# One ring of four two-bank PSUM tiles in the first attention, and each head's output in its own half of the array

## The chip, the cores and the metric

The kernel runs on one core of a Trainium2 chip. The metric is the device time of one launch in microseconds (us). Before the change it is 3492.91 us (median of three runs, 3492.39 to 3498.04).

The engines have short names in the profile: PE is TensorE's matmuls, PEld its weight loads, DVE VectorE, ACT ScalarE, POOL GpSimd, SP the engine that issues the DMAs. PSUM is TensorE's output memory: eight banks, each 512 float32 columns over 128 partitions.

## The reference

One inference step of two layers, each an attention and a squared-ReLU MLP, for a prompt of 1024 tokens and for 8 samples of 8 new tokens with paged caches. The change concerns the first attention over the prompt. Cut to what matters (16 query heads of 64 channels share 2 key/value heads; three branches: compressed rows, all earlier rows, the last 512 rows):

```python
s = jnp.einsum('btkgd,bckd->bkgtc', qg, kc)               # compressed: at most 64 columns
p_cmp = softmax(where(c_ok, s, NEG)); o_cmp = einsum('bkgtc,bckd->btkgd', p_cmp, vc)
...                                                        # selected: top 16 of 16 blocks, causal
p = softmax(where(ok, s, NEG)); o_sel = einsum('bkgtnj,bktnjd->btkgd', p, vg)
s = jnp.einsum('btkgd,bckd->bkgtc', qg, kw)               # window: the last 512 rows
p = softmax(where(ok_w, s, NEG)); o_win = einsum('bkgtc,bckd->btkgd', p, vw)
g = gates.reshape(B, Tq, Hk, G, 3)
out = o_cmp * g[..., 0:1] + o_sel * g[..., 1:2] + o_win * g[..., 2:3]
```

## The kernel before

The stage is the method `nsa_prompt`. It works on 8 pairs of heads `p`, and in each pair on 8 block rows `i` of 128 queries, in the order 0, 7, 1, 6, 2, 5, 3, 4. A unit (p, i) has two parts.

`scores(p, i)` computes for each of the two heads the scores of the three branches with float32 matmuls into PSUM tiles `S` of two banks (one tile for i below 3, else two), takes each branch's maximum on VectorE (L675), exponentiates on ScalarE into an SBUF tile `P` (L678, the last reader of `S`), takes a reciprocal (L682) and scales `P` by reciprocal and gate on GpSimd (L685).

`values(p, i)` multiplies `P` by the values. The product contracts over keys, so each block of 128 columns of `P` is first transposed on TensorE (L109), for both heads, into a PSUM tile `tr` of one bank that holds two blocks of both heads; one copy per tile, alternately on VectorE and ScalarE (the call at L714, recorded at L98 and L96), moves it to the SBUF tile `PT`. A block row has 3, 5, 7, 9, 11, 12, 13 or 14 blocks (i = 0 to 7), 74 per pair. The value matmuls (L726, recorded at L106) use 64 of the 128 columns of the array: a matmul takes one block's values as weights and streams both heads' 256 columns, and successive blocks go to the lower and the upper half of the array, which accumulate in the two halves of the partitions of a tile `av` of [128, 256]. So the two halves hold two partial sums: ScalarE copies the lower one to `oh` (L729), and VectorE adds the upper one, a head at a time (L731), into `oT`. A float32 matmul is recorded as two passes; "x24" in a row are 24 such records.

`prep(p+1)` transposes the queries of the next pair (L625) and splits them into two parts (`X`).

The PSUM tiles come from three pools of two (L614): `Sp` 2 x 2 banks, `trp` 2 x 1, `avp` 2 x 1, eight banks in all. A pool gives its tiles in turn; a tile's first writer waits until the last reader of the tile that had its place is done, and instructions on one tile wait for each other as far as they are of different engines and at least one writes.

The generators of all units are run in an interleaved order set by `stagger`, from start and length given for each at the end of the function (`ng` is the number of steps of `values`); every engine then runs its instructions in program order.

Of the kernel before, what the change touches and what calls it, by code (L numbers as in the profile page):

```python
# [12 lines left out]
AF = mybir.ActivationFunctionType  # L13
OP = mybir.AluOpType
AX = mybir.AxisListType
PSUM = bass.MemoryType.PSUM
# [55 lines left out]
class Step:  # L72
# [534 lines left out]
    def nsa_prompt(self, oT):  # L607
        nc, io = self.nc, self.io
        cmN, A, B, V = self.cmN, self.A, self.B, self.V
        with ExitStack() as ctx:  # L610

            qp = self.pool(ctx, bufs=2, side="right")
            sp = self.pool(ctx)
            Sp, trp, avp = (self.pool(ctx, bufs=2, space=PSUM) for _ in range(3))  # L614
            st = {}

            def prep(p):
                k = p // 4
                X = [(sp if p % 2 else qp)("X", [128, NP], F32R, bufs=2) for _ in range(2)]
                st[p] = X  # L620
                qn = qp("qn", [128, 8, 128])
                nc.sync.dma_start(qn, self.zq[0:NP, p * 128:p * 128 + 128].rearrange("(t p) c -> p t c", p=128))
                for g in range(2):
                    cs = slice(g * 512, g * 512 + 512)
                    ps = trp("tr", [128, 512]) if p else Sp("S", [128, 1024])[:, 0:512]  # L625
                    for i in range(4):
                        self.tr(ps[:, i * 128:i * 128 + 128], qn[:, 4 * g + i, :], 128)
                    for s in range(2):
                        self.qk_prep(ps, s * 64, X[s][k * 64:k * 64 + 64, cs], X[s][64 - k * 64:128 - k * 64, cs])
                        yield  # L630
# [59 lines left out]
            def scores(p, i):  # L690
                for s in range(2):
                    yield from score(p, i, s)

            def values(p, i):


                k = p // 4
                ks = slice(k * 64, k * 64 + 64)
                P, w1, j0 = zip(*(st[p, i, s] for s in range(2)))
                w1, j0 = w1[0], j0[0]  # L700

                blocks = [(0, V[0][:, ks])]
                blocks += [(64 + j * 128, V[1][:, j, ks]) for j in range(i + 1)]
                blocks += [(64 + w1 + (j - j0) * 128, V[2][:, j, ks]) for j in range(j0, i + 1)]
                nb = len(blocks)
                PT = sp("PT", [128, 14, 2, 128], bufs=2)
                for x0, x1 in [(max(x, 0), x + 2) for x in range(-(nb % 2), nb, 2)]:
                    ps = trp("tr", [128, 2, 2, 128])
                    for x in range(x0, x1):
                        for s in range(2):  # L710
                            o = blocks[x][0]
                            last = self.tr(ps[:, x - x0, s], P[s][:, o:o + 128], 128)
                    self.n_p += 1
                    self.hi("va"[self.n_p % 2], PT[:, x0:x1], ps[:, 0:x1 - x0])  # L714
                    yield
                av = avp("av", [128, 256])
                todo = [(x, None) for x in range(nb - 1, nb % 2 - 1, -1)] + [(0, s) for s in range(2) if nb % 2]
                with self.tc.issue_after(last.ins):
                    for c, (x, s) in enumerate(todo):
                        h = slice(c % 2 * 64, c % 2 * 64 + 64)  # L720
                        y = PT[:, x] if s is None else PT[:, x, s]
                        if s is None:
                            o, y = av[h], y.rearrange("p a b -> p (a b)")
                        else:
                            o = av[h, s * 128:s * 128 + 128]
                        self.mm(o, blocks[x][1], y, c < 2, c >= len(todo) - 2)  # L726
                yield
                oh = sp("oh", [64, 256], bufs=2)
                nc.scalar.activation(oh, av[0:64], AF.Copy)  # L729
                for s in range(2):  # L730
                    nc.vector.tensor_tensor(oT[p][s * 64:s * 64 + 64, i * 128:i * 128 + 128],  # L731
                                            av[64:128, s * 128:s * 128 + 128], oh[:, s * 128:s * 128 + 128], OP.add)

            units = [(p, i) for p in range(8) for i in (0, 7, 1, 6, 2, 5, 3, 4)]
            gens = [(-1, 1, 4, prep(0))] + [(8 * p + 0.5, 7, 4, prep(p + 1)) for p in range(7)]
            for u, (p, i) in enumerate(units):
                ng = (i + 1 + min(i + 1, 5) + 2) // 2
                gens.append((u, 1, 4 if i < 3 else 8, scores(p, i)))
                gens.append((u + 1.2, 1, ng + 1, values(p, i)))
            stagger(gens)  # L740
# [813 lines left out]
```

## Time and profile before

| | |
|---|---|
| median of three runs | 3492.91 us |
| the profiled execution | 3498.1 us, its span 3496.3 us |
| mean granted clock of TensorE over the span | 0.986 |
| the stage `nsa_prompt` | from 480.8 to about 1011 us of the span, 65.3 us per pair |
| TensorE busy in 476 to 1012 us | 499.9 of 536 us |
| VectorE, ScalarE, GpSimd busy there | 361.9, 355.0, 246.8 us |

A row of the groups reads: source line, engine, operation, output<-input by the program's names, shapes, count | busy us, mean ns of one | idle time of the engine just before, and what ended it. A helper that all stages share has one line: L106 is the matmul, L109 the transposition, L96 and L98 the copies on ScalarE and VectorE. A matmul's recorded duration includes the time until its last column is out; the step from one start to the next is the rate.

### The profile page before, as it was taken

The numbers are of one execution on the slowest core, as the hardware profiler recorded it, in microseconds if no ns is written. First come the engines' busy times: TensorE is split into PE (matmuls) and PEld (weight loads), VectorE is DVE, ScalarE is ACT, GpSimd is POOL, SyncE is SP. The second block draws the span as 40 slices with busy tenths as digits, with TensorE's granted clock in tenths as the row PEclk, the third lists the DMA queues.
The fourth block names the chain that finished last, engine by engine and source line by source line (L and its number), as shares of the span: only waits on it lengthen the run. The fifth ranks groups of instructions, "written<-read, shape, count | busy, mean of one in ns | idle before, by whom it ended". The sixth has DMA issues, their size and how long they took to land.

```text
span 3496.3 us, 57244 instructions
## 1 busy us (share of the span) xinstructions
PE 3361.6 (96%) x21901; PEld 2827.9 (81%) x21901; DVE 1934.7 (55%) x4109; ACT 1233.5 (35%) x3084; POOL 746.2 (21%) x1036
## 2 busy tenths in 40 slices
PE   7999989999999999999999999899989999999998
PEld 5879756666679999999998777667669999999998
DVE  4356566766665444445447213777775544444445
ACT  6223466666653111111114221667763211111111
POOL 0242234444430011100004203222230100111102
PEclk9999999999999999999999999999999999999999
DMA  7433420000012111111113222666631211111111
GB/s 222 146 91 98 139 64 7 7 13 1 1 65 75 34 49 49 49 43 43 36 37 116 94 94 89 216 220 224 203 100 56 60 49 31 49 49 49 43 37 52
DMA packets 242380, 270.88 MB, mean 77 GB/s; under 512 B 23930, under 2 KB 190970, under 8 KB 242042
## 3 DMA queue, kind: packets, MB, share of 16 engines
q1 hardware_dynamic: 242106, 267.23, 24.4%
q8 instruction: 172, 2.82, 0.3%
q14 instruction: 102, 0.84, 0.1%
HBM read 229.81 MB, written 41.50 MB: 78 GB/s over the span
## 4 chain that ended last, share of the span: by engine, by line
PE 83%; DVE 6%; ACT 5%; DMA 2%; SPq 2%; issue 1%; POOL 0%; DVEq 0%; ACTq 0%; POOLq 0%
PE dn L106 26%; PE up L106 22%; PE ps L106 12%; PE av L106 7%; PE S L106 6%; PE tr L109 6%; PE hid L106 2%; ACT P L678 2%; PE tr L106 1%; DVE ml L675 1%; SPq L142 1%; DVE PT L98 1%; DVE hl L242 0%; DVE oT L103 0%; DVE oT L731 0%
## 5 line engine op out<-in xcount | busy, mean ns | idle before, releaser
L1061 DVE TENSOR_TENSOR xT<-xT,dn 128x512 f32<-128x512 f32 (+2 forms) x768 | 404.0, 530 | 497.5 <-PE dn L106 496.6
L106 PE MATMUL dn<-xh,dh 128*128 128x512 f32 (+2 forms) x1536 | 504.5, 328 | 0.6 <-DVE xT L1061 0.6
L106 PE MATMUL up<-hh,uh 128*128 128x512 f32 (+2 forms) x1536 | 503.9, 328 | 1.2 <-DVE u L1037 1.2
L106 PE MATMUL dn<-xl,dh 128*128 128x512 f32 (+2 forms) x1536 | 504.7, 329 | 0.0
L106 PE MATMUL dn<-xh,dl 128*128 128x512 f32 (+2 forms) x1536 | 503.4, 328 | 0.0
L106 PE MATMUL up<-hh,ul 128*128 128x512 f32 (+2 forms) x1536 | 502.8, 327 | 0.0
L106 PE MATMUL up<-hl,uh 128*128 128x512 f32 (+2 forms) x1536 | 502.4, 327 | 0.0
L99 POOL TENSOR_SCALAR xh<-u 128x512 fp32r<-128x512 f32 (+2 forms) x192 | 142.8, 744 | 1309.5 <-PE dn L106 858.6
L1038 ACT ACTIVATE u<-u 128x512 f32<-128x512 f32 (+2 forms) x192 | 96.5, 502 | 829.3 <-DVE u L1037 827.3
L106 PEld LDWEIGHTS up<-hh,uh 128*128 128x128 f32 x1536 | 289.7, 189 | 25.1 <-DVE u L1037 1.8
L106 PEld LDWEIGHTS up<-hl,uh 128*128 128x128 f32 x1536 | 289.7, 189 | 22.3
L106 PEld LDWEIGHTS up<-hh,ul 128*128 128x128 f32 x1536 | 289.6, 189 | 22.2
L106 PEld LDWEIGHTS dn<-xh,dh 128*128 128x128 f32 x1536 | 289.5, 188 | 21.5 <-DVE xT L1061 1.0
L106 PEld LDWEIGHTS dn<-xh,dl 128*128 128x128 f32 x1536 | 289.2, 188 | 21.6
L106 PEld LDWEIGHTS dn<-xl,dh 128*128 128x128 f32 x1536 | 289.5, 188 | 19.9
L685 POOL TENSOR_SCALAR P<-P,ml,gates 128x64 f32<-128x64 f32 (+8 forms) x384 | 244.5, 652 | 281.8 <-DVE ml L682 254.8
L106 PE MATMUL ps<-wh,hh 128*128 128x512 f32 (+2 forms) x720 | 278.7, 388 | 9.5 <-ACT wh L96 7.4
L106 PE MATMUL S<-A,X 128*128 128x512 f32 (+7 forms) x608 | 250.5, 412 | 29.4 <-ACT P L678 22.4
L106 PE MATMUL ps<-wh,hl 128*128 128x512 f32 (+2 forms) x720 | 277.5, 387 | 0.0
L106 PE MATMUL ps<-wl,hh 128*128 128x512 f32 (+2 forms) x720 | 277.4, 386 | 0.1
L109 PE MATMUL tr<-ident,P 128*128 128x128 f32 (+1 forms) x1584 | 245.9, 282 | 19.4 <-DVE PT L98 6.8
L678 ACT ACTIVATE P<-S,ml 128x64 f32<-128x64 f32 (+8 forms) x384 | 216.3, 571 | 84.1 <-DVE ml L675 65.0
(311 smaller groups left out, 6386.4 us busy)
## 6 DMA issues: line engine op xcount, KB each, us to landing
ur<-in_mlp_w_up_dram SPq DMA_DIRECT2D x64, 512.0 KB
dr<-in_mlp_w_down_dram SPq DMA_DIRECT2D x64, 512.0 KB
kt<-in_cache_diff_kv_dram SPq DMA_DIRECT2D x64, 512.0 KB
vt<-in_cache_diff_kv_dram SPq DMA_DIRECT2D x64, 512.0 KB
ur<-in_diff_w_in_dram SPq DMA_DIRECT2D x24, 512.0 KB
xT<-x_saved SPq DMA_DIRECT2D x16, 544.0 KB
nat<-in_cache_nsa_cmp_dram SPq DMA_DIRECT2D x128, 64.0 KB
zq<-ro SPq DMA_DIRECT2D x32, 256.0 KB
```

The source lines that it names most:

```text
L98: return self.nc.vector.tensor_copy(out, x)
L99: return self.nc.gpsimd.tensor_scalar(out, x, 1.0, 0.0, op0=OP.mult, op1=OP.add)
L106: self.nc.tensor.matmul(out, lhsT, rhs, start=start, stop=stop)
L109: return self.nc.tensor.transpose(out, x, self.ident[:n, :n])
L142: self.page_dmas.append(self.nc.sync.dma_start(out, in_))
L675: nc.vector.tensor_reduce(nm[:, br:br + 1], x, AX.X, OP.max, negate=True)
L678: nc.scalar.activation(P[:, c:c + x.shape[1]], x, AF.Exp, bias=nm[:, br:br + 1], accum_out=l[:, br:br + 1])
L685: nc.gpsimd.tensor_scalar(P[:, c0:c1], P[:, c0:c1], l[:, br:br + 1], g[:, br:br + 1], op0=OP.mult, op1=OP.mult)
L1038: nc.scalar.activation(u[:, :w], u[:, :w], AF.Square)
L1061: nc.vector.tensor_tensor(x, x, ps[:, :w], OP.add)
```

## The change

The three pools become one, `Sp`, a ring of four tiles of two banks. Out of it come, in program order, the score tiles, the query transpositions of `prep`, the transpositions of `values`, and the outputs.

- A transposition tile holds four blocks of both heads, one pair of blocks in each bank; each bank has its copy as before.
- The output tile is [128, 128]: the product of head 0 goes to the lower, that of head 1 to the upper half of the array, each with 128 streamed columns per block and all blocks accumulated in the one half. One VectorE copy of 128x128 moves it to `oT`. `oh`, its ScalarE copy and the two additions are gone.
- `ng` counts groups of four blocks now.

```diff
-            Sp, trp, avp = (self.pool(ctx, bufs=2, space=PSUM) for _ in range(3))
+
+            Sp = self.pool(ctx, bufs=4, space=PSUM)
...
-                    ps = trp("tr", [128, 512]) if p else Sp("S", [128, 1024])[:, 0:512]
+                    ps = Sp("S", [128, 1024])[:, 0:512]
...
-                for x0, x1 in [(max(x, 0), x + 2) for x in range(-(nb % 2), nb, 2)]:
-                    ps = trp("tr", [128, 2, 2, 128])
-                    for x in range(x0, x1):
+                for x0 in range(0, nb, 4):
+                    ps = Sp("S", [128, 1024]).rearrange("p (x s c) -> p x s c", x=4, s=2)
+                    for y0 in range(x0, min(x0 + 4, nb), 2):
+                        y1 = min(y0 + 2, nb)
+                        for x in range(y0, y1):
+                            for s in range(2):
+                                o = blocks[x][0]
+                                last = self.tr(ps[:, x - x0, s], P[s][:, o:o + 128], 128)
+                        self.n_p += 1
+                        self.hi("va"[self.n_p % 2], PT[:, y0:y1], ps[:, y0 - x0:y1 - x0])
+                    yield
+                av = Sp("S", [128, 1024])[:, 0:128]
+                with self.tc.issue_after(last.ins):
+                    for x in range(nb - 1, -1, -1):
                         for s in range(2):
-                            o = blocks[x][0]
-                            last = self.tr(ps[:, x - x0, s], P[s][:, o:o + 128], 128)
-                    self.n_p += 1
-                    self.hi("va"[self.n_p % 2], PT[:, x0:x1], ps[:, 0:x1 - x0])
-                    yield
-                av = avp("av", [128, 256])
-                todo = [(x, None) for x in range(nb - 1, nb % 2 - 1, -1)] + [(0, s) for s in range(2) if nb % 2]
-                with self.tc.issue_after(last.ins):
-                    for c, (x, s) in enumerate(todo):
-                        h = slice(c % 2 * 64, c % 2 * 64 + 64)
...
-                        self.mm(o, blocks[x][1], y, c < 2, c >= len(todo) - 2)
+                            self.mm(av[s * 64:s * 64 + 64], blocks[x][1], PT[:, x, s], x == nb - 1, x == 0)
+                nc.vector.tensor_copy(oT[p][:, i * 128:i * 128 + 128], av)
                 yield
-                oh = sp("oh", [64, 256], bufs=2)
-                nc.scalar.activation(oh, av[0:64], AF.Copy)
-                for s in range(2):
-                    nc.vector.tensor_tensor(oT[p][s * 64:s * 64 + 64, i * 128:i * 128 + 128],
-                                            av[64:128, s * 128:s * 128 + 128], oh[:, s * 128:s * 128 + 128], OP.add)
...
-                ng = (i + 1 + min(i + 1, 5) + 2) // 2
+                ng = (i + 1 + min(i + 1, 5) + 1 + 3) // 4
```

Place 1 is TensorE's order at block row 7 of the second pair: the end of its scores and its transpositions (`tr<-ident,P` before, `S<-ident,P` after, since the tiles come from the ring; the name in brackets is the engine waited for). Before:

```order
L109 MATMUL tr<-ident,P 128x128 [waits Activation_49]
L109 MATMUL tr<-ident,P 128x128 x3
L106 MATMUL S<-A_6227,X 128x512 [waits Activation_49]
L106 MATMUL S<-B_6228,X 128x512
L106 LDWEIGHTS identb
L106 MATMUL S<-masks,identb 128x128
L106 MATMUL S<-A_6227,X 128x128
L106 MATMUL S<-B_6228,X 128x128
L106 LDWEIGHTS identb
L106 MATMUL S<-masks,identb 128x128
L109 MATMUL tr<-ident,P 128x128 [waits DVE_49]
L109 MATMUL tr<-ident,P 128x128 x3
```

After:

```order
L109 MATMUL S<-ident,P 128x128 [waits Pool_49]
L109 MATMUL S<-ident,P 128x128 x7
L109 MATMUL S<-ident,P 128x128 [waits Pool_49]
L109 MATMUL S<-ident,P 128x128 [waits PE_49,Activation_49]
L109 MATMUL S<-ident,P 128x128 x3
L109 MATMUL S<-ident,P 128x128 [waits Activation_49]
L109 MATMUL S<-ident,P 128x128 x3
L109 MATMUL S<-ident,P 128x128 [waits Activation_49]
L109 MATMUL S<-ident,P 128x128 x3
L109 MATMUL S<-ident,P 128x128 [waits Activation_49]
L109 MATMUL S<-ident,P 128x128 x3
L106 MATMUL S<-A_5690,X 128x512 [waits DVE_49]
```

Before, groups of four transpositions stand between score tiles. After, the first halves of four tiles and then the second halves of three stand together, each second half behind a wait for ScalarE, and the next score tile behind a wait for VectorE.

Place 2 is TensorE's order at block row 2 of the second pair (7 blocks), from its last transpositions to its value products; the numbers are those of the buffers. Before:

```order
L109 MATMUL tr_7963<-ident_65,P_7850 128x128 [waits DVE_49,Pool_49]
L109 MATMUL tr_7963<-ident_65,P_7902 128x128 [waits Pool_49]
L109 MATMUL tr_7963<-ident_65,P_7850 128x128
L109 MATMUL tr_7963<-ident_65,P_7902 128x128
L109 MATMUL tr_7974<-ident_65,P_7850 128x128 [waits DVE_49]
L109 MATMUL tr_7974<-ident_65,P_7902 128x128
L109 MATMUL tr_7974<-ident_65,P_7850 128x128
L106 MATMUL av_7951<-PT_7878,V2_6225 64x256 [waits Activation_49]
L106 MATMUL av_7951<-PT_7878,V2_6225 64x256 x2
L106 MATMUL av_7951<-PT_7878,V1_5688 64x256 x3
L106 MATMUL av_7951<-PT_7878,vcp_2290 64x128 x2
```

After:

```order
L106 MATMUL S_8005<-A20_6227,X_6796 128x128
L106 MATMUL S_8005<-B20_6228,X_6796 128x128
L106 LDWEIGHTS identb_69
L106 MATMUL S_8005<-masks_71,identb_69 128x128
L109 MATMUL S_7996<-ident_65,P_7832 128x128 [waits DVE_49]
L109 MATMUL S_7996<-ident_65,P_7875 128x128
L106 MATMUL S_8018<-PT_7966,V2_6225 64x128 [waits Activation_49]
L106 MATMUL S_8018<-PT_7966,V2_6225 64x128 x5
L106 MATMUL S_8018<-PT_7966,V1_5688 64x128 x6
L106 MATMUL S_8018<-PT_7966,vcp_2290 64x128 x2
```

Before, seven transpositions of the next block row stand between the copies and the products that read them. After, the products stand directly behind the last two transpositions, and wait for ScalarE, which copies these.

## Rows read from the trace of the kernel before

**Rows 1.** The page, part 1: busy time, share of the span, instructions

```profile
PE 3361.6 (96%) x21901; PEld 2827.9 (81%) x21901; DVE 1934.7 (55%) x4109; ACT 1233.5 (35%) x3084; POOL 746.2 (21%) x1036
```

**Rows 2.** Windows, a pair and the stage; us by engine, then clock, DMA, GB/s

```profile
611.00:677.00 66.00, 62.41 (x483) 44.42 (x485) 44.94 (x106) 44.56 (x135) 31.40 (x51) 1.00 0.03 9
...
476.00:1012.00 536.00, 499.86 (x3881) 355.96 (x3880) 361.93 (x846) 354.97 (x1043) 246.76 (x387) 0.99 0.02 7
```

**Rows 3.** The waits in the stage: us in total, times, longest us

```profile
PEld S L106 <- ACT P L678: 35.4, 55, 1.4
...
PEld tr L109 <- DVE PT L98: 9.2, 11, 1.0
...
PEld tr L109 <- ACT PT L96: 5.0, 7, 0.9
...
DVE oT L731 <- ACT oh L729: 59.4, 42, 2.9
```

**Rows 4.** Groups by form on TensorE: busy us, mean ns, idle before

```profile
L106 PE MATMUL av<-PT,V 128*64 128x256 f32 x1056 | 133.0, 386 | 1.4 <-DVE PT L98 1.4
...
L106 PE MATMUL av<-PT,vcp 128*64 128x128 f32 x192 | 18.6, 273 | 0.0
...
L109 PE MATMUL tr<-ident,P 128*128 128x128 f32 x1187 | 176.3, 279 | 9.9 <-DVE PT L98 6.5 <-ACT PT L96 3.3
```

**Rows 5.** The groups by form on VectorE in the stage

```profile
L675 DVE TENSOR_REDUCE ml<-S 128x1 f32<-128x1024 f32 x16 | 19.6, 1224 | 10.0 <-PE S L106 9.0 <-POOL P L685 1.0
...
L675 DVE TENSOR_REDUCE ml<-S 128x1 f32<-128x640 f32 x80 | 64.9, 818 | 9.7 <-PE S L106 8.7
...
L675 DVE TENSOR_REDUCE ml<-S 128x1 f32<-128x64 f32 x128 | 28.1, 219 | 26.8 <-PE S L106 25.9
...
L731 DVE TENSOR_TENSOR oT<-av,oh 64x128 f32<-64x128 f32 x128 | 37.6, 294 | 61.6 <-ACT oh L729 59.4
```

**Rows 6.** The groups by form on ScalarE in the stage

```profile
L96 ACT ACTIVATE PT<-tr 128x512 f32<-128x512 f32 x136 | 81.0, 595 | 31.0 <-PE tr L109 29.3
...
L678 ACT ACTIVATE P<-S,ml 128x1024 f32<-128x1024 f32 x16 | 17.9, 1118 | 2.8 <-DVE ml L675 2.8
...
L678 ACT ACTIVATE P<-S,ml 128x640 f32<-128x640 f32 x80 | 63.5, 793 | 8.7 <-DVE ml L675 7.8
...
L678 ACT ACTIVATE P<-S,ml 128x64 f32<-128x64 f32 x128 | 40.0, 312 | 57.5 <-DVE ml L675 40.2 <-PE tr L109 12.9 <-PE S L106 1.4
...
L729 ACT ACTIVATE oh<-av 64x256 f32<-64x256 f32 x64 | 24.1, 376 | 39.6 <-PE av L106 39.2
```

**Rows 7.** Tiles named av, later stage: ns shortest/mean/longest, where in the span

```profile
L1266 DVE COPY oT<-av x64: 259/290/293, 2213.9 to 2606.9; 128x128 f32<-128x128 f32 x64
```

**Rows 8.** Timeline, values of block row 2: start, us, idle and releaser

```profile
724.28 0.71 PE L109 MATMUL tr<-ident,P 128*128 128x128 f32 x5
...
725.03 0.69 DVE L98 COPY PT<-tr 128x512 f32<-128x512 f32 x1
...
725.78 0.55 PE L109 MATMUL tr<-ident,P 128*128 128x128 f32 x3 [0.79 <-DVE PT L98]
```

**Rows 9.** The timeline, a score tile of 640 columns and the next

```profile
713.74 0.48 PE L106 MATMUL S<-A,X 128*128 128x512 f32 x1
...
714.66 0.61 PE L109 MATMUL tr<-ident,P 128*128 128x128 f32 x4
...
716.16 0.50 PE L106 MATMUL S<-A,X 128*128 128x512 f32 x1 [0.90 <-ACT P L678]
```

**Rows 10.** The timeline, value products and transpositions

```profile
644.30 0.39 PE L106 MATMUL av<-PT,vcp 128*64 128x128 f32 x4
...
644.62 1.09 PE L109 MATMUL tr<-ident,P 128*128 128x128 f32 x8
...
653.31 2.81 PE L106 MATMUL av<-PT,V 128*64 128x256 f32 x24
```

**Rows 11.** The timeline, value products of 64 columns in the stage before

```profile
433.93 0.69 PE L106 MATMUL av<-PT,kv 128*64 128x64 f32 x16
```

More of the change, by code (lines that the diff above doesn't have):

```diff
@@ L716, in values @@
-                av = avp("av", [128, 256])
-                todo = [(x, None) for x in range(nb - 1, nb % 2 - 1, -1)] + [(0, s) for s in range(2) if nb % 2]
-                with self.tc.issue_after(last.ins):
-                    for c, (x, s) in enumerate(todo):
-                        h = slice(c % 2 * 64, c % 2 * 64 + 64)
[L721 to L725, printed above, removed]
-                        self.mm(o, blocks[x][1], y, c < 2, c >= len(todo) - 2)
```

## The prediction

> **What bounds the kernel now.** First the busy times: over the span TensorE works 96% of the time, VectorE 55%, ScalarE 35% [rows 1]. Then the windows of the one stage that the change touches. In its 536 us TensorE is busy 499.9 at a granted clock of 0.99, so 36.1 us are idle; VectorE (361.9), ScalarE (355.0) and GpSimd (246.8) have a third or more of it free [rows 2]. One pair of heads has the same shares [rows 2]. The stage is therefore TensorE's order plus its stalls, and what another engine saves counts only where TensorE waits for it. Third, the waits: TensorE's weight loads wait 35.4 us in 55 pieces for ScalarE's exponentials, which release score tiles, 9.2 us for VectorE's copies of transpositions and 5.0 us for ScalarE's. The sum is 49.6 us, 6.2 per pair; it exceeds the idle time since a weight load can wait while earlier matmuls still run. The largest wait of all, 59.4 us, is VectorE's for `oh` [rows 3], on a chain that no row shows TensorE waiting for.
>
> **Work removed and added.**
>
> Value products. Before there are 1056 + 32 records of 256 columns and 192 of 128; after 592 blocks x 2 heads x 2 passes = 2368 of 128; the two large groups of before have their rows [rows 4]. A 256-column record costs (2.81 - 0.38)/23 = 0.106 us from start to start, less the length of the last; for 128 columns, four in 0.39 and the change of shape behind them in 0.32, which leaves 0.04 to 0.055 [rows 10]. At half of 0.106: 1088 x 0.106 + 192 x 0.053 = 125.5 before, 2368 x 0.053 = 125.5 after. The work is the same. Twice as many records need twice as many weight loads; the floor that these set is below (0.69 - 0.24)/15 = 0.030 per record, the rate of 64 columns [rows 11], so I add nothing.
>
> The Trainium skill, "TensorEngine Tiling (Array Packing)", Instruction Overhead, gives each matmul about 60 cycles of its own; at the clock of these rows that would make 1088 more records some 27 us dearer, as an estimate. The trace speaks against it: 128 columns cost half of 256 here.
>
> Copies. 64 ScalarE copies (24.1 us) [rows 6] and 128 VectorE additions (37.6) [rows 5] go; 64 copies of 128x128 come, 0.290 each by the same form in a later stage [rows 7], 18.6 us. That is 24 us less of ScalarE and 19 of VectorE. Both have more idle time than this, so it counts at zero directly; indirectly it shortens the queue in which exponentials and transposition copies stand, which is in the walk below.
>
> Changes of shape. A change from 128-wide matmuls to 64-wide costs about 0.10 us, and as much back: after the last of four 128-column products the transposition starts 0.32 after the first, where four steps of 0.053 make 0.21 [rows 10]. I count the stretches of value products in the order of one pair: 9 before, 11 after. 2 x 2 x 0.10 x 8 = **+3 us**.
>
> The Trainium skill, "TensorEngine Tiling (Array Packing)", Key Properties, says that a change of tiling mode drains the engine; the 0.10 agrees.
>
> Ends of the stage. At the start the eight query transpositions of the first pair now stand behind the last value products of the stage before, not among them; at the end the last output waits for one copy, not for a copy and an addition (0.376 + 0.294 against 0.290). I take **+1** for both. Single-block stretches of the products, which could not pair with one of the other half before: **+1**.
>
> **The waits, walked.** The change makes a transposition tile two banks, so its second half waits for the copy of its first half, and the value products and scores draw from the same four tiles. A pair needs 26 score tiles, 22 transposition tiles, 8 outputs and 2 query tiles: 58 in 65.3 us, so a tile lives 4.5 us if all four are in use.
>
> The price of a wait comes from one row: four transpositions end their steps at 724.83 (five from 724.28 at 0.11), VectorE's copy runs from 725.03 for 0.69, and the next group starts at 725.78 [rows 8]. So a group that waits for a VectorE copy of the group right before it loses 0.95 us, and for a ScalarE copy (0.595, [rows 6]) 0.86. With PE work D between, the loss is 0.95 - D or 0.86 - D, plus what the copy waits in its own queue. In the order of one pair before, 30 waits of transpositions or products for a copy have D of 0.89 or more but for one; after there are 21, of which 12 have D under 1.1, six of these 0.87 (two groups), and two value products D = 0. That is the core of the forecast: fewer waits, and closer ones.
>
> I went through one pair after the change by hand, with durations from the rows [rows 4 to 10], an instruction starting when its engine and its waits allow. The losses in us:
>
> - Block row 7 (place 1), 3.1. The ring is full of first halves that wait. Its second head's tiles, of 1024 and of 640 + 64 columns, come 1.04 us apart (a tile of 640 takes 714.66 - 713.74 = 0.92 for 1536 columns in all, [rows 9]). The second scores tile of block row 1 waits until the later one is exponentiated: the reduction of 1024 (1.224, [rows 5]), then exponentials of 1.118, 0.793 and 0.312 [rows 6] and 0.2 of accumulator reads, about 2.5 after the scores. TensorE has products (0.5), a tile of block row 1 (0.9) and two transpositions (0.2) meanwhile: 0.9 lost. The next transposition tile waits for three more exponentials (0.31 and twice 0.47, between the rows of 64 and 640): 0.6. Three second halves wait for ScalarE copies that follow each other at 0.6 against 0.44 of transpositions: 0.3; GpSimd's scaling 0.16. The next two score tiles wait for exponentials behind only ten transpositions (1.09) where the same chain needs 2.2: 1.15.
> - Block rows 1 and 6, 1.4 and 0.74, of the same two kinds.
> - Block row 2, 1.1: the products directly behind the last transpositions (place 2) lose 0.86 less the 0.10 of the change of shape, 0.75; a first half's copy behind a reduction 0.35.
> - Block row 5, 0.9 (products again 0.78), 3, 0.75, and 4, 0.35.
>
> Together 8.3 us per pair if successive VectorE instructions overlap as the trace mostly shows, 9.65 if they run end to end. Before, 6.2. So +2.1 to +3.4 per pair, 8 pairs: +17 to +28; I take **+22**.
>
> Where the waits could be less than walked: the engines may run ahead in ways that a walk by means misses, and the scores' waits before (35.4 us) are all up for removal by a deeper ring, which bounds the gain at about 30 us. Where more: every second half that pays the full 0.95.
>
> Sum: 22 + 3 + 1 + 1 = +27 on the profiled execution's 3498.1, 3525. That execution is 5.2 above the median of the three runs, so the median comes to **3520**.
>
> The Trainium skill, "PSUM — Partial Sum Buffer", PSUM bank collisions raise a hardware error, forbids two engines on the same bank and partitions only; by it TensorE could fill a tile's second bank while the first is copied. The order after makes it wait all the same, as the brackets of place 1 show.
>
> **Rivals.**
>
> - R1, faster. The ring of four is what scores needed: a block row's two heads have four score tiles, before only two could stand. If the 35.4 us of waits for exponentials go to about 5 and the second halves stay hidden behind neighbouring groups, the stage loses some 30 us: 3493 - 30 + 4 = 3467. For it: this wait is by far the largest and ScalarE loses 24 us of work. Against: transposition tiles hold ring places for two copies each, and three in five of the ring's tiles are not scores.
> - R2, an even exchange: the score waits that go pay for the second halves that come, 3493.
> - R3, slower by more. The second halves mostly wait as in rows 8: 18 tiles per pair have a second half; if each loses 0.4 net of the score waits that go, under half of the 0.95, 18 x 0.4 x 8 = 58 come on top of 3493, with the small terms 3555 at most; I take 3550. It decides if copies stand behind reductions and exponentials in the queues, which have 67% load.
> - That the change does not do what it says is excluded for the products (the order shows 64x128 and one copy) and for the ring.
>
> **How the numbers follow.** Forecast 0.56 (its own range 3503 to 3536, from the walk's ends and 5 us of the small terms), R1 0.18, R2 0.13, R3 0.13. A difference under 0.2%, 7 us, can't be told from no change. Faster: R1 and a part of R2, 0.20; within: most of R2 and the forecast's lower tail, 0.13; slower 0.67. The range leaves out most of R1 below and half of R3's upper tail: 3484 to 3547.
>
> **What would show it.** Right: in the windows of the stage about 27 us more, all of it in TensorE's idle time, with its busy time as before; in the waits, the transpositions' row for VectorE and ScalarE copies together above 25 us, and a row of value products for a copy of some 10 to 15. The waits of scores for exponentials should stay above 20. The step on the products is wrong if the mean of their 128-column records differs much from 273 ns or TensorE's busy time moves by over 5 us; the walk is wrong if the score waits fall below 10 us or the second halves' waits are under 10.

## The result, and the profile after

The changed kernel takes 3527.14 us (median of four runs, 3524.91 to 3528.41) against 3495.47 before (four runs): a ratio of 1.0088, 95% interval 1.0074 to 1.0103, slower by about 31 us. The forecast was 3520.

The profiled execution after takes 3524.9 us, its span 3523.1. The difference lies in the stage. Counted from the first score matmul to the first matmul of the output projection, it lasts 527.3 us before (480.83 to 1008.17) and 558.7 after (479.60 to 1038.30), 31.4 more. The rest of the span is 4.6 us shorter, less than executions of one kernel differ by (before 3492.39 to 3499.11).

The window of the stage after, longer by the 27 us of the two spans, answers to [rows 2] (PE, PEld, DVE, ACT, POOL busy, clock, DMA share, GB/s):

```profile
476.00:1039.00 563.00, 509.96 (x4929) 398.24 (x4925) 336.91 (x778) 327.36 (x972) 246.31 (x385) 1.00 0.03 7
```

TensorE's idle time there is 53.0 us and not 36.1, at a granted clock of 1.00 (before 0.99). The two windows take in unlike pieces of the neighbouring stages, so here is the stage between its own bounds, before and after:

```profile
480.83:1008.17 527.34, 492.45 (x3800) 350.08 (x3800) 355.67 (x836) 348.53 (x1026) 244.51 (x384) 0.99 0.02 7
...
479.60:1038.30 558.70, 507.05 (x4888) 396.20 (x4888) 334.73 (x768) 325.22 (x961) 245.95 (x384) 1.00 0.03 7
```

TensorE is idle 16.8 us more and busy 14.6 us more; VectorE is busy 20.9 us less and ScalarE 23.3. The waits of the window of 563 us answer to [rows 3] (us in total, times, longest; an `S` stands now for scores, transpositions and outputs, so L109 is a transposition, L106 a score or a product; PEld is a weight load that waits):

```profile
DVE oT L723 <- PE S L106: 57.9, 41, 3.0
...
PEld S L106 <- ACT P L679: 28.6, 32, 1.6
...
PEld S L106 <- ACT PT L96: 14.6, 16, 1.0
...
PEld S L109 <- ACT P L679: 12.0, 23, 0.7
...
PEld S L106 <- DVE PT L98: 8.1, 17, 1.5
...
PEld S L109 <- DVE PT L98: 4.6, 16, 0.5
...
PEld S L109 <- ACT PT L96: 2.6, 9, 0.8
```

Scores wait less for exponentials (28.6, before 35.4), but transpositions now wait for them too (12.0), since they take their places from the same ring. Transpositions wait less for copies: 4.6 + 2.6, before 9.2 + 5.0. Up from 3.0 + 0.5 (before, under `av`) are the 14.6 + 8.1 us in which matmuls of L106 wait for copies. Whose they are is in the groups, which answer to [rows 4]:

```profile
L109 PE MATMUL S<-ident,P 128*128 128x128 f32 x1184 | 171.3, 280 | 12.7 <-ACT P L679 8.2 <-DVE PT L98 2.0 <-POOL P L686 1.4
L106 PE MATMUL S<-PT,V 128*64 128x128 f32 x2112 | 134.5, 277 | 19.5 <-ACT PT L96 10.8 <-DVE PT L98 7.2 <-ACT P L679 1.3
...
L106 PE MATMUL S<-PT,vcp 128*64 128x128 f32 x256 | 24.9, 273 | 0.0
```

In front of the value products TensorE is idle 19.5 us, before 1.4: 18.1 more, where its idle time grew by some 17 in all. One such place in the timeline, which answers to [rows 8]:

```profile
673.19 0.64 PE L109 MATMUL S<-ident,P 128*128 128x128 f32 x4
...
673.46 0.96 DVE L676 TENSOR_REDUCE ml<-S 128x1 f32<-128x64 f32 x2
...
673.87 0.60 ACT L96 ACTIVATE PT<-S 128x512 f32<-128x512 f32 x1 [0.55 <-PE S L109]
...
674.52 0.88 PE L106 MATMUL S<-PT,V 128*64 128x128 f32 x12 [0.69 <-ACT PT L96]
```

The last four transpositions of a block row are followed at once by its products. These begin with the blocks that were transposed last, so they wait for the copy of the group right before them: 0.96 us from the start of the last transposition (673.56) to the first product.

Busy and idle time of TensorE mix a little, since a matmul's record runs on while its last columns come out (a transposition's lasts 0.28 us, and the next one starts after 0.11). So the table below counts from the start of each matmul to the start of the next over the stage, and sorts these steps by what comes next. The four columns make up the whole stage; the last one includes the step from the last product to the output projection, 0.2 to 0.8 us and in e2 4.0. Each row is one execution, the profiled one; those of e3 and e7 were 7 and 5 us below their kernels' medians. All figures are us; "into products" is what passes between another matmul and the first of a stretch of products, with the number of stretches.

| kernel | stage | product to product | into products | into transpositions | into scores |
|---|---|---|---|---|---|
| before | 527.3 | 121.8 | 15.0 (71) | 160.5 | 230.1 |
| after | 558.7 | 124.8 | 37.0 (87) | 163.3 | 233.6 |
| e1_own_half | 522.1 | 125.6 | 15.1 (70) | 152.5 | 228.9 |
| e2_ring_only | 576.9 | 134.7 | 37.8 (80) | 176.1 | 228.2 |
| e3_first_first | 539.6 | 125.0 | 16.4 (82) | 170.8 | 227.3 |
| e4_two_blocks | 550.1 | 125.9 | 35.4 (64) | 152.4 | 236.4 |
| e5_steps_of_four | 507.4 | 125.3 | 18.7 (77) | 149.1 | 214.2 |
| e7_transpositions_three | 496.4 | 125.9 | 12.7 (65) | 142.3 | 215.5 |
| e11_eight_then_copies | 557.7 | 125.5 | 50.5 (73) | 152.2 | 229.5 |
| e12_two_blocks_first_first | 546.9 | 125.4 | 13.8 (80) | 164.8 | 242.8 |

After against before: 22.0 of 31.4 us stand in front of the products, 3.0 between them, 2.8 and 3.5 in front of the rest.

### The profile page after: what moved, and what is told of

Same layout as the page of the kernel before. It is cut to its first block, busy times and chain, and to the rows that moved or that the text cites. A ratio compares the mean times of both kernels' runs of the same rounds, so it can differ in the third digit from the quotient of the medians.

```text
span 3523.1 us, 59378 instructions
## 1 busy us (share of the span) xinstructions
PE 3375.6 (96%) x22989; PEld 2875.7 (82%) x22989; DVE 1914.4 (54%) x4045; ACT 1210.0 (34%) x3020; POOL 749.1 (21%) x1036
## 4 chain that ended last, share of the span: by engine, by line
PE 83%; DVE 7%; ACT 4%; DMA 2%; issue 2%; SPq 2%; POOL 0%; DVEq 0%; ACTq 0%; POOLq 0%
PE dn L106 26%; PE up L106 22%; PE ps L106 12%; PE S L106 10%; PE tr L109 4%; PE av L106 3%; PE S L109 3%; DVE ml L676 2%; PE hid L106 2%; SPq L142 1%; ACT P L679 1%; PE tr L106 1%; DMA ur<-in_nsa_w_in_dram 1%; DVE PT L98 1%; DVE hl L242 0%
## 5 line engine op out<-in xcount | busy, mean ns | idle before, releaser
L106 PE MATMUL dn<-xh,dh 128*128 128x512 f32 (+2 forms) x1536 | 504.6, 328 | 0.7 <-DVE xT L1053 0.7
L106 PE MATMUL up<-hh,uh 128*128 128x512 f32 (+2 forms) x1536 | 503.8, 328 | 1.2 <-DVE u L1029 1.2
L106 PE MATMUL dn<-xl,dh 128*128 128x512 f32 (+2 forms) x1536 | 504.6, 329 | 0.0
L106 PE MATMUL dn<-xh,dl 128*128 128x512 f32 (+2 forms) x1536 | 503.4, 328 | 0.0
L106 PE MATMUL up<-hh,ul 128*128 128x512 f32 (+2 forms) x1536 | 502.8, 327 | 0.0
L106 PE MATMUL up<-hl,uh 128*128 128x512 f32 (+2 forms) x1536 | 502.4, 327 | 0.0
L106 PEld LDWEIGHTS up<-hh,uh 128*128 128x128 f32 x1536 | 289.7, 189 | 25.1 <-DVE u L1029 1.8
L106 PEld LDWEIGHTS up<-hl,uh 128*128 128x128 f32 x1536 | 289.7, 189 | 22.3
L106 PEld LDWEIGHTS up<-hh,ul 128*128 128x128 f32 x1536 | 289.6, 189 | 22.2
L106 PEld LDWEIGHTS dn<-xh,dh 128*128 128x128 f32 x1536 | 289.6, 189 | 21.5 <-DVE xT L1053 1.0
L106 PEld LDWEIGHTS dn<-xh,dl 128*128 128x128 f32 x1536 | 289.2, 188 | 21.6
L106 PEld LDWEIGHTS dn<-xl,dh 128*128 128x128 f32 x1536 | 289.5, 188 | 19.8
L106 PE MATMUL ps<-wh,hh 128*128 128x512 f32 (+2 forms) x720 | 278.3, 388 | 8.9 <-ACT wh L96 7.2
L106 PE MATMUL ps<-wh,hl 128*128 128x512 f32 (+2 forms) x720 | 277.4, 387 | 0.0
L106 PE MATMUL ps<-wl,hh 128*128 128x512 f32 (+2 forms) x720 | 277.4, 387 | 0.0
L106 PE MATMUL S<-A,X 128*128 128x512 f32 (+7 forms) x608 | 252.1, 415 | 23.6 <-ACT P L679 15.3
L676 DVE TENSOR_REDUCE ml<-S 128x1 f32<-128x64 f32 (+8 forms) x384 | 193.4, 540 | 89.1 <-PE S L106 86.5
```

Source lines behind the costliest of these rows:

```text
L106: self.nc.tensor.matmul(out, lhsT, rhs, start=start, stop=stop)
L676: nc.vector.tensor_reduce(nm[:, br:br + 1], x, AX.X, OP.max, negate=True)
```

## The experiments

Each kernel below was timed beside the kernel before on the same chip, and its ratio goes by that. A step is one turn of a unit's generator in the interleaved order. The theory at the start (A) was that the loss is the wait in front of the products; the rivals were dearer 128-column products (B) and waits for places in the shared ring (C).

**e1_own_half: the products alone**

```diff
-                av = avp("av", [128, 256])
+                av = avp("av", [128, 128])
...
+                    for x in range(nb - 1, -1, -1):
+                        for s in range(2):
+                            self.mm(av[s * 64:s * 64 + 64], blocks[x][1], PT[:, x, s], x == nb - 1, x == 0)
+                nc.vector.tensor_copy(oT[p][:, i * 128:i * 128 + 128], av)
```

> The old three pools and the old one-bank transposition tiles; of the change only the products: each head in its own half, one VectorE copy of 128x128. Theory A (the loss is TensorE waiting in front of the value products for the copies of transpositions issued just before them, which the four-block tiles bring about): no loss here, 3495 within 6 us, and the value products' idle time in front of them stays near the 1.4 us of before. Rival B (128-column products are dearer in themselves, by weight loads or by what each record costs): the busy-time part of the loss, 8 to 14 us, shows here, 3503 to 3509. If freeing ScalarE and VectorE pays anything, it is below 3489.

Measured: 3489.0 us, ratio 0.9989 (0.9979 to 0.9999). The idle time in front of the products stays at 1.4:

```profile
L109 PE MATMUL tr<-ident,P 128*128 128x128 f32 x1184 | 171.5, 278 | 7.5 <-DVE PT L98 7.1 <-ACT PT L96 0.2
L106 PE MATMUL av<-PT,V 128*64 128x128 f32 x2112 | 130.9, 276 | 1.4 <-DVE PT L98 1.4
```

So this half of the change does no harm with the old pools; it pays about 4 us, within its interval some 0 to 7. By the table the products themselves cost 3.8 more, and 8.0 come back in front of the transpositions. Their wait for ScalarE's copies is down to 0.8 from 5.0; that for VectorE's is as before:

```profile
PEld tr L109 <- DVE PT L98: 9.9, 12, 1.0
...
PEld tr L109 <- ACT PT L96: 0.8, 2, 0.4
```

That ScalarE no longer has the outputs' copies is the likely reason, and was not tried by itself. B falls: the products are 3.8 us dearer, not 8 to 14.

**e2_ring_only: the ring with the old products**

```diff
-                av = Sp("S", [128, 1024])[:, 0:128]
+                av = Sp("S", [128, 1024])[:, 0:256]
...
+                oh = sp("oh", [64, 256], bufs=2)
+                nc.scalar.activation(oh, av[0:64], AF.Copy)
```

The products and the two additions are as before, too.

> The ring of four with transposition tiles of four blocks as after the change, but the products as before: 256 columns, blocks alternating between the halves, a ScalarE copy and two additions. Theory A: nearly the whole loss is here, 3520 to 3530, with about 20 us of idle time in front of the value products. Rival B: 3512 to 3519, the ring's part alone. If the copies and additions now delay the release of ring tiles, it is above 3530.

Measured: 3540.0 us, ratio 1.014 (1.0123 to 1.0157). The ring holds the whole loss and some 13 to 18 us more (by the medians and by the ratios), above the range of every theory but the last clause, that the copies and additions delay the release of ring tiles. The reason given there shows little: TensorE stands idle for the additions 1.5 us in front of transpositions, and 3.7 at the stage's end. What grows against after the change are the transpositions' weight loads' waits for exponentials (21.6, after 12.0) and the idle time in front of the products (28.0, after 19.5):

```profile
L109 PE MATMUL S<-ident,P 128*128 128x128 f32 x1184 | 173.7, 282 | 20.8 <-ACT P L679 15.7 <-DVE PT L98 2.4 <-DVE oT L733 1.5
L106 PE MATMUL S<-PT,V 128*64 128x256 f32 x1056 | 142.7, 386 | 28.0 <-DVE PT L98 15.5 <-ACT PT L96 11.1 <-ACT P L679 1.3
```

Both are waits for ScalarE and VectorE, which in e2 still have the outputs' copies and additions. The run does not separate these from the form of the products.

**e3_first_first: the products from the first block to the last**

```diff
-                    for x in range(nb - 1, -1, -1):
+                    for x in range(nb):
...
-    self.mm(av[s * 64:s * 64 + 64], blocks[x][1], PT[:, x, s], x == nb - 1, x == 0)
+    self.mm(av[s * 64:s * 64 + 64], blocks[x][1], PT[:, x, s], x == 0, x == nb - 1)
```

> After the change, but the products go through the blocks from the first to the last, so that the blocks copied last are multiplied last. Theory A: the wait in front of the products goes from about 20 us to about 5, as the last copies run beside the first products; 3510 to 3516. Rival C (the loss is in the shared ring, where scores and transpositions wait for tiles): the wait only changes its place, 3523 to 3530.

Measured: 3511.0 us, ratio 1.0058 (1.0041 to 1.0074). A third to half of the loss (11 us by the ratios, 16 by the medians) is gone with the order of one loop, as A has it:

```profile
L109 PE MATMUL S<-ident,P 128*128 128x128 f32 x1184 | 170.5, 279 | 21.4 <-ACT P L679 8.1 <-ACT PT L96 4.8 <-POOL P L686 4.7
L106 PE MATMUL S<-PT,V 128*64 128x128 f32 x2112 | 130.2, 273 | 0.0
...
L106 PE MATMUL S<-PT,vcp 128*64 128x128 f32 x256 | 28.1, 298 | 1.8 <-ACT P L679 1.6 <-DVE PT L98 0.2
```

The idle time in front of the products is 1.8 us, less than the 5 that were expected. It stands before the compressed rows' products (`vcp`), which now come first, and 1.6 of it is for a place in the ring. Some of what is saved turns up in front of the transpositions (21.4, after 12.7). By the table 20.6 are saved in front of products and 6.3 of scores, and 7.5 are lost again. What remains, 18 to 20 us over before, is not the products' wait.

**e4_two_blocks: two blocks to a ring tile**

```diff
-                for x0 in range(0, nb, 4):
-                    ps = Sp("S", [128, 1024]).rearrange("p (x s c) -> p x s c", x=4, s=2)
+                for x0, x1 in [(max(x, 0), x + 2) for x in range(-(nb % 2), nb, 2)]:
+                    ps = Sp("S", [128, 1024])[:, 0:512].rearrange("p (x s c) -> p x s c", x=2, s=2)
...
-                ng = (i + 1 + min(i + 1, 5) + 1 + 3) // 4
+                ng = (i + 1 + min(i + 1, 5) + 2) // 2
```

> After the change, but a transposition tile holds two blocks again (half of a ring tile stays unused) with a step of the interleaving for each, as before the change: 74 ring tiles per pair and not 58, no second halves. Theory A: the copies get distance from the products again, so the idle time in front of them falls below 8 us; the time is 3500 to 3512, as the ring turns faster. Rival C: more tiles through four places make the waits for places longer, 3530 to 3550.

Measured: 3520.2 us, ratio 1.0082 (1.0065 to 1.0098); neither range holds it. The products' wait does not go with the four-block tiles. It is as long (21.9, after the change 19.5): its part for copies is down to 11.9 us from 18.0, and 9.3 us of it are now for a place in the ring (ACT P):

```profile
L106 PE MATMUL S<-PT,V 128*64 128x128 f32 x2112 | 129.4, 275 | 21.9 <-DVE PT L98 9.6 <-ACT P L679 9.3 <-ACT PT L96 2.3
```

So A was right on where the time stands and mostly wrong on the four-block tiles as its cause.

**e5_steps_of_four: the old pools, steps of four blocks**

```diff
-                for x0, x1 in [(max(x, 0), x + 2) for x in range(-(nb % 2), nb, 2)]:
-                    ps = trp("tr", [128, 2, 2, 128])
+                for x0 in range(0, nb, 4):
+                    for y0 in range(x0, min(x0 + 4, nb), 2):
+                        ps = trp("tr", [128, 2, 2, 128])
...
-                ng = (i + 1 + min(i + 1, 5) + 2) // 2
+                ng = (i + 1 + min(i + 1, 5) + 1 + 3) // 4
```

The diff is against e1.

> As e1_own_half (old pools, one-bank tiles, own halves), but a step of the interleaving issues four blocks' transpositions (two one-bank tiles), as after the change. Theory A1 (the coarse steps bring the last transpositions next to the products, whatever pool they are from): 10 to 20 us of idle time in front of the products return, 3500 to 3509. Rival A2 (it is the shared ring, in whose turn transpositions wait for places until just before the products): as e1, 3485 to 3493, under 5 us there.

Measured: 3473.9 us, ratio 0.9931 (0.9914 to 0.9947). A1 falls: the coarse steps alone are a gain of 15 to 20 us on e1, with 4.3 us idle in front of the products. A2 is right about the products, and missed the gain, which is in front of the scores (214.2 by the table, e1 228.9); their weight loads wait 19.2 us for exponentials, in e1 35.0:

```profile
L106 PE MATMUL av<-PT,V 128*64 128x128 f32 x2112 | 132.5, 276 | 4.3 <-DVE PT L98 4.2
...
PEld S L106 <- ACT P L678: 19.2, 43, 0.9
```

**e6_scores_three: a third place for scores**

```diff
-            Sp, trp, avp = (self.pool(ctx, bufs=2, space=PSUM) for _ in range(3))
+            Sp, trp = (self.pool(ctx, bufs=n, space=PSUM) for n in (3, 2))
...
-                av = avp("av", [128, 128])
+                av = trp("tr", [128, 512])[:, 0:128]
```

The diff is against e1.

> Own halves; scores get three two-bank places, transpositions and products share two one-bank places. It tries what one more place for scores is worth by itself: the 34 us that score tiles wait for exponentials. If they are worth what they take: 3460 to 3470. If the transpositions, with two places shared with the products, take the wait over: 3495 to 3520, with waits of transpositions for copies and for the output's copy above 40 us. I hold the second for likelier.

Measured: 3562.0 us, ratio 1.0184 (1.0167 to 1.0201), worse than the second case. The scores' wait for exponentials is nearly gone, 2.7 us of 35. Far more comes back in front of the products and transpositions, which share two places now; the gain and the price of the one edit can't be told apart:

```profile
PEld tr L106 <- ACT PT L96: 57.6, 47, 1.5
PEld tr L109 <- DVE PT L98: 24.1, 38, 1.0
PEld tr L109 <- ACT PT L96: 22.8, 37, 0.9
PEld tr L106 <- DVE PT L98: 15.2, 13, 1.3
...
PEld S L106 <- ACT P L678: 2.7, 5, 1.7
```

**e7_transpositions_three: a third place for transpositions**

```diff
-            Sp, trp, avp = (self.pool(ctx, bufs=2, space=PSUM) for _ in range(3))
+            Sp, trp, avp = (self.pool(ctx, bufs=n, space=PSUM) for n in (2, 3, 1))
```

The diff is against e1.

> As e1_own_half, but one bank moves from the outputs to the transpositions: places 2 x 2 banks for scores, 3 x 1 for transpositions, 1 for outputs. If the third place takes away the 16 us of transpositions waiting for copies: 3472 to 3482. If these are set by the score waits around them, or one place for outputs makes the products wait for the last output's copy: 3485 to 3495.

Measured: 3463.8 us, ratio 0.9912 (0.9896 to 0.9929): the best of all kernels, 31 us under before. The outputs keep one place where they had two, and the products hardly wait for it (1.2 us, and that for copies). The transpositions get it; their wait is all but gone, and that of the scores is down from 35.0 in e1 to 20.2, though scores have no place more:

```profile
PEld S L106 <- ACT P L678: 20.2, 47, 1.4
...
PEld av L106 <- DVE PT L98: 1.2, 2, 1.0
...
PEld tr L109 <- ACT PT L96: 0.9, 1, 0.9
...
PEld tr L109 <- DVE PT L98: 0.4, 2, 0.3
```

**e8_outputs_apart: a ring of three, outputs outside it**

```diff
-            Sp = self.pool(ctx, bufs=4, space=PSUM)
+            Sp, avp = (self.pool(ctx, bufs=n, space=PSUM) for n in (3, 2))
...
-                av = Sp("S", [128, 1024])[:, 0:128]
+                av = avp("av", [128, 128])
```

> After the change, but outputs have two one-bank places of their own and the ring is three tiles of two banks for scores and four-block transpositions. Theory A1 (steps and four-block tiles): the wait in front of the products stays at 15 to 22 us, and one place less in the ring costs more: 3530 to 3550. Rival A2 (products queue in the ring): it falls below 8 us, 3510 to 3525.

Measured: 3579.8 us, ratio 1.024 (1.0223 to 1.0257). Neither theory: the products hardly wait (1.2 us idle, as A2 said), and the time is the worst of all. One place less for scores and transpositions together costs more than the products' wait did:

```profile
PEld S L106 <- ACT P L679: 35.4, 39, 2.0
PEld S L106 <- ACT PT L96: 32.5, 46, 1.0
PEld S L109 <- DVE PT L98: 24.7, 45, 1.3
PEld S L109 <- ACT P L679: 15.9, 17, 1.5
PEld S L109 <- POOL P L686: 13.9, 30, 1.3
```

**e9_three_and_steps: e5 and e7 together**

```diff
-            Sp, trp, avp = (self.pool(ctx, bufs=2, space=PSUM) for _ in range(3))
+            Sp, trp, avp = (self.pool(ctx, bufs=n, space=PSUM) for n in (2, 3, 1))
```

The diff is against e5.

> e7_transpositions_three and e5_steps_of_four together: own halves, places 2 x 2 for scores, 3 x 1 for transpositions, 1 for outputs, steps of four blocks. If the two gains (31 and 21 us against before) have one source, the distance between a copy and what waits for it, they overlap: 3455 to 3466. If they are of different places they add: 3440 to 3454. If one place for outputs meets products that come sooner after each other, it is above e7.

Measured: 3474.4 us, ratio 0.9947 (0.9931 to 0.9964), above both e7 and the first range. The gains don't add. The last clause has the time but not the reason: the products wait 1.2 us. Transpositions hardly wait in either kernel. In front of the scores e9 has 6.0 us more than e7, of the 8.8 us by which its stage is longer (505.2 and 496.4); their weight loads wait 23.8 us for exponentials, in e7 20.2. Another 4.1 us stand in front of the products, in 80 stretches and not 65. Why the steps that helped with two places hurt with three stays open.

**e10_outputs_with_transpositions: a ring without scores**

```diff
-            Sp, trp, avp = (self.pool(ctx, bufs=2, space=PSUM) for _ in range(3))
+            Sp, trp = (self.pool(ctx, bufs=n, space=PSUM) for n in (2, 4))
...
-                av = avp("av", [128, 128])
+                av = trp("tr", [128, 512])[:, 0:128]
```

The diff is against e1.

> As e7_transpositions_three with steps of two, but outputs and transpositions share one pool of four one-bank places: a ring, but one without scores. Theory A3 (what costs is that scores, which hold a place for reduction and exponentials, some 3 to 4 us, and transpositions, which hold it for one copy, take places of the same ring in turn, so that the short ones wait behind the long ones): no loss here, 3455 to 3470. Rival A4 (any sharing of the outputs with the transpositions costs, as in e6_scores_three): 3490 to 3530, with products or transpositions waiting for copies above 20 us.

Measured: 3476.4 us, ratio 0.9946 (0.9929 to 0.9963). A4 falls: it is 13 to 15 us faster than e1, with 2.0 us idle in front of the products. It ends 6 us above A3's range, and sharing is not free: e7 divides the same four banks into three places and one, and is 12 to 13 us faster. Its scores wait less for exponentials (20.2 us, here 29.3); why was not tried.

```profile
L106 PE MATMUL tr<-PT,V 128*64 128x128 f32 x2112 | 129.4, 276 | 2.0 <-DVE PT L98 1.8
...
PEld S L106 <- ACT P L678: 29.3, 47, 1.4
```

A ring of outputs and transpositions alone is thus far from the loss of the ring that has the scores in it, too.

**e11_eight_then_copies: no second half waits**

```diff
-                        self.n_p += 1
-                        self.hi("va"[self.n_p % 2], PT[:, y0:y1], ps[:, y0 - x0:y1 - x0])
+                    for y0, y1 in ys:
+                        self.n_p += 1
+                        self.hi("va"[self.n_p % 2], PT[:, y0:y1], ps[:, y0 - x0:y1 - x0])
```

> After the change, but all eight transpositions of a tile stand before its two copies, so that no second half waits for the copy of the first half; the place itself is held as before. If the second halves' waits are the cost that the prediction made them: a large part of the 31 us comes back, 3495 to 3508. If the trace of after is right, in which transpositions wait only 7 us for copies: 3518 to 3532, with the score and place waits unchanged and the products' wait as large.

Measured: 3523.5 us, ratio 1.0087 (1.007 to 1.0104), as without the edit. What the transpositions gain (152.2 by the table, after 163.3) the products lose:

```profile
L109 PE MATMUL S<-ident,P 128*128 128x128 f32 x1184 | 163.2, 278 | 5.4 <-ACT P L679 2.3 <-POOL P L686 2.1
L106 PE MATMUL S<-PT,V 128*64 128x128 f32 x2112 | 131.4, 276 | 35.7 <-DVE PT L98 20.1 <-ACT PT L96 15.5
```

Without the second half's wait the same copies are late for the products, so removing it gains nothing. The edit also issues the first half's copy only after the second half's transpositions, so it does not price that wait by itself; that it is small is in the 7.2 us that all transpositions wait for copies after the change.

**e12_two_blocks_first_first: e3 and e4 together**

```diff
-                    for x in range(nb - 1, -1, -1):
+                    for x in range(nb):
...
-    self.mm(av[s * 64:s * 64 + 64], blocks[x][1], PT[:, x, s], x == nb - 1, x == 0)
+    self.mm(av[s * 64:s * 64 + 64], blocks[x][1], PT[:, x, s], x == 0, x == nb - 1)
```

The diff is against e4.

> e4_two_blocks with the products going from the first block to the last as in e3_first_first. In e4 24 us of TensorE's start-to-start time stand in front of the products, about 12 of them for copies and 9 for a place in the ring. If the copies' part goes and the place stays: 3506 to 3512. If the products' wait goes altogether: 3496 to 3503. If the ring is no dearer than three pools once the order of the products is mended: 3486 to 3494, as e1_own_half.

Measured: 3513.8 us, ratio 1.0053 (1.0036 to 1.0071), just above the first range and well above the others. The products' wait is gone (0.1 us, and 0.4 before the compressed rows' products, which come first), and most of it stands elsewhere: the place that the products waited for is now waited for by transpositions and scores.

```profile
PEld S L106 <- ACT P L679: 32.0, 55, 1.8
...
PEld S L109 <- ACT P L679: 7.5, 10, 0.9
PEld S L109 <- POOL P L686: 7.2, 28, 0.7
PEld S L109 <- DVE oT L721: 6.6, 9, 0.8
PEld S L109 <- ACT PT L96: 5.8, 14, 0.5
```

Against e1, which has the same steps and products but for their direction, the stage is 24.8 us longer: 12.3 in front of transpositions, 13.9 of scores. By the medians it is 25 us, by the ratios 22. This is what the ring of four costs when hardly anything waits in front of the products.

## Why the prediction was right in its sum, and where its steps were not

The sum was +27 on the profiled execution, whose span grew by 26.8; the medians differ by 31.7. That the two agree to 0.2 us is luck: the stage grew by 31.4 and the rest shrank by 4.6. The sign and the rough size are earned, since the added stalls of TensorE in this stage are the larger part of it. Two of the signs that the prediction named failed: the additional time was to be idle time alone, and 14.6 us of it are busy time; and the transpositions' waits for copies are 7.2 us, under the 10 at which the walk was to be called wrong. By its own steps:

- **Copies at zero.** The work saved is as summed: VectorE 20.9 us less where 19 were counted, ScalarE 23.3 where 24 were. What it is worth was put into the walk without a term of its own, and it is not nothing: with the old pools 8.0 us come back in front of transpositions (e1), and in the ring the own halves as a whole save 13 to 18 us (e2 against after).
- **Products at zero.** The rate was right to 3 us: 121.8 between products before, 124.8 after, 125.6 in e1, with the mean of a 128-column record at 277 ns. The Trainium skill's 60 cycles of overhead for a matmul ("TensorEngine Tiling (Array Packing)", Instruction Overhead), taken as added to each, would have been 27 us here, as an estimate; the measurement, 3.0 us, decides against it.
- **Changes of shape.** 71 stretches became 87; 72 and 88 were counted. From the last transposition to the first product with nothing to wait for it is 0.20 us, between transpositions 0.11, as taken: about +3.
- **The walk**, +17 to +28. In the sum it is at the lower end, and its parts do not hold: TensorE's idle time grew by 16.8 us, 2.1 per pair. The walk set losses of TensorE after (8.3 to 9.65 per pair) against waits of weight loads before (6.2), which run longer than the idle time that they cause; in idle time alone it is 4.4 per pair before and 6.5 after. Its core was that second halves stand close behind the copies of first halves. The transpositions' waits for copies were to be above 25 us; they are 7.2, half of what they were before (14.2), and e11, which has no second halves' waits, is no faster. The products' wait was put at two places per pair, some 12 us in all, and expected to read 10 to 15; it is 19.5 idle, 22.0 more than before from start to start. Two errors of opposite sign cancelled in part. The close waits of transpositions hardly came about; why, by groups of other tiles between or by copies that came sooner, was not followed in the trace. And the products waited behind their last transpositions at more block rows than the two that the walk priced: 35 of the 87 stretches follow a transposition directly, half of these 0.86 us or more after its start, where before it was 47 of 71, half of them at 0.20.
- **Scores' waits above 20 us.** Right, 28.6. But the ring's transpositions wait 12.0 us for exponentials as well, so that exponentials are waited for 40.6 us and not 35.4.
- **TensorE's busy time as before, within 5 us.** Wrong: 10.1 more in the two windows, 14.6 in the stage. By the prediction's words this would convict the products, but e1, which has them, is busy 2.6 us less than before (489.9 and 492.5). 3.0 are between products; the rest goes with the additional stalls and changes of shape, as the end of a record counts as busy until its last column is out. TensorE stands idle 115 times in the stage, before 72; at 0.17 us for each (0.28 less 0.11) this is 7 us, and the 16 more stretches at 0.2 are 3. That is an estimate from the rows, not tried.

R1, the gain by a deeper ring for scores, fails by its condition: the waits for exponentials did not go to 5 us. What they would be worth alone isn't shown, since e6, which removes nearly all of them and is 67 us slower, takes the outputs' places for it. R3's second halves did not wait as it needed (7.2 us in all). R2's even exchange did not come about: the scores' waits hardly went (28.6, before 35.4), and without the products' wait, which it did not have either, 18 to 20 us of the loss remain (e3).

**What stays open.** e3 puts a third to half of the loss, 11 to 16 us, on the order of the products. The rest is in the ring, as e12 against e1 shows. Two things come together in it and were not taken apart: that the tiles are given out in one turn, so that a transposition can stand behind a score tile which is held through reduction and exponentials, and that four places of two banks replace six places, an output taking a whole one for 128 of its 1024 columns and, in e12, a transposition tile one for 512. No run joins e3's order with e11's late copies, and none has e7's places with the old products.

## What to carry to other kernels

Count a pool's places, and not its banks alone: one ring of four large tiles lost 22 to 25 us to six places of fitting size (e12 against e1), and one bank moved from the outputs to the transpositions brought 25 to 27 (e7 against e1). Start an accumulation with the operand that is ready first; beginning with the last one copied let TensorE wait for that copy, 11 to 16 us here (e3). And when a walk gives the right sum, check its parts against the waits: here one part was some 18 us too high and another some 10 too low.

## What was not expected of the hardware

Little in the engines: the 64-wide products' records start in pairs 7 ns apart, at 256 columns as at 128, and the next pair 0.21 us later at 256 and 0.10 at 128, so that a pair of 128 columns takes half of a pair of 256. Unexpected is how little a saved wait says: e6 removes 32 us of one wait and loses 67, and e8 removes 18 and loses 53 against the kernel after.
